# One transformer layer on one core: the forward retention states move from the attention loop into the last projection chunk, with a new order of the first instructions and of the query tiles

## The chip, the cores and the metric

The program runs on one core of a Trainium2 chip. The metric is device time in microseconds (us) of one execution; the value for a kernel is the median of its runs. PE is the matrix engine (TensorE), DVE the vector engine, ACT the scalar engine, POOL GpSimd, and SP the engine whose queue issues all DMAs here.

## The reference, cut to what matters

One layer over 2048 rows of width 1024 with a context of 256 rows. All products of activations and weights are made from pairs of float16 parts (a high and a low one, three matmuls for one), and the retention products in float32.

```python
h = modulate(rmsnorm(x)); hc = modulate(rmsnorm(ctx))
rq, rk, rv, rg, aq, ak, av = split(h @ w_in)          # 6 column chunks of w_in
# retention, 4 heads, chunks of 128 rows, forward and backward:
scores = einsum('id,jd->ij', q, k) * intra
o      = scores @ v + (q @ state) * q_dec
state  = state * c_dec + (k * k_dec).T @ v            # one update for each chunk
ret = groupnorm(o_forward + o_backward) * silu(rg)
att = softmax(q @ k_all.T) @ v_all                    # 8 query heads on 2 key heads, keys: 18 tiles of 128
x = x + g1 * (concat(ret, att) @ w_out)
x = x + g2 * (square(relu(modulate(rmsnorm(x)) @ w_ff1)) @ w_ff2)
out = rmsnorm(x) * final_norm_g
```

## The kernel before, in words

**Three stages.** A projection stage, an attention stage and a feed-forward stage follow each other. The change touches the first and the beginning of the second.

**Projection stage.** Each engine takes its instructions in the order in which the program emits them, and that order is written out by hand: `at(q, step, fn)` files a call under a half-row `q` and one of eight steps (`dma`, `mm`, `turn`, `copy`, `work`, `mix`, `extra`, `store`), and a loop at the end emits the calls by `q` and step. A row is one tile of 128 rows of activations (2 context tiles, 16 latent tiles) times one column chunk of `w_in`: 24 matmuls, 12 in each of two half-rows. The chunks come in the order value (18 rows), key (18), attention key and value (18, half as wide), attention query (16), gate (16), retention query (16). `base[col]` is the first half-row of a chunk; in the code the chunks' first half-rows are also called `rk`, `akv`, `aq`, `rg`, `rq`. Beside the rows the plan holds:

- the normalised activations, each tile once, in the value chunk (`load_x`, `squares`, `root`, `normal`, then `turn_h`, `modulate`, `high_h`, `low_h` for each half). The first tiles are made ahead of the loop, beside the modulation vectors that the first part of `w_mod` gives (`mods`, `modulation`)
- `later_rows`: the rest of the modulation vectors, on DVE, with eight float32 sums on PE
- `maxima`: the greatest weights of the later matrices, on DVE (`w_ff1`) and ACT (the others)
- `decay_tables`: the retention's decay factors, `value_parts`: the float16 parts of the values, `ff_scales`: scales for the later stages
- `first_maxima`: for the first three groups of the attention, 18 `piece` matmuls each into the PSUM tag `mp` (two buffers) and 18 `maximum` reductions on DVE

**Attention stage.** It runs over steps `k`; a list of phases (`begin`, `scores`, `piece`, `maximum`, `early`, `exp`, `cast`, `low`, `chain`, `pe`, `values`, `late`, `dma`) orders what a step emits. A group is a tile of 128 queries with one key head, 32 groups of 18 steps, from the last tile (15) to the first. A step scores one tile of keys, takes exponentials on ACT, splits them into float16 parts (ACT, then POOL or DVE) and multiplies by the values. The scores of the first group start at step 22. Group 3 is the first whose pieces and maxima are made in this stage, from step 54.

**Retention.** `retention(24)` files its work into the attention's steps. From step 24, every two steps, it makes one state: 17 forward chunks (`d` = 0), then two backward ones. For each of them `take` loads a key and a value tile of 256 KB each, `weigh` multiplies the keys by their decay on POOL, `product` makes four float32 matmuls into a PSUM bank, and `update` combines them with the old state in four DVE instructions; `keep_state` stores forward states to DRAM for later use (two buffers, tag `sf`). From step `R0` = 66, every 35 steps, one retention tile and one output tile are made.

Of the kernel before, what the change touches and what calls it, by code (L numbers as in the profile page):

```python
# [55 lines left out]
def layer_kernel(ctx: ExitStack, tc: tile.TileContext, a: dict, out: bass.AP):  # L56
# [205 lines left out]
    with ExitStack() as st:  # L262
# [212 lines left out]
        for m in range(3, len(TILES)):  # L475
            q = 2 * (m - 3)
            if m > 3:
                at(max(0, q - 6), "dma", load_x, m)
                at(max(0, q - 3), "copy", squares, m)
                at(max(0, q - 2), "work", root, m)  # L480
                at(max(1, q - 1), "mix", normal, m)
# [92 lines left out]
        class Row:  # L574


            def __init__(self, s):
# [26 lines left out]
                elif self.col == C_AQ:  # L604
# [8 lines left out]
                    at(q + 3, "turn", self.turn)  # L613
                    at(q + 4, "copy", self.split_turned)
                    at(q + 5, "store", self.store_turned, aq_d)
                else:
# [11 lines left out]
                    at(q + 6, "turn", self.turn_key)  # L628
                    at(q + 7, "work", self.keep_key)
# [301 lines left out]
        def decay_tables(q0):  # L931
# [10 lines left out]
            def rates():  # L942
# [4 lines left out]
                nc.scalar.activation(u, lr, AF.Exp)  # L947
                nc.vector.tensor_scalar(w1, u, -1.0, 1.0, op0=ALU.mult, op1=ALU.add)
                nc.scalar.activation(ln, w1, AF.Ln)
                nc.vector.tensor_scalar(z, u, -1.0, 2.0, op0=ALU.mult, op1=ALU.add)  # L950
                nc.vector.reciprocal(z, z)
                nc.vector.tensor_mul(z, z, u)
                nc.vector.tensor_mul(zz, z, z)
                nc.vector.tensor_scalar(lg, zz, 1.0 / 17, 1.0 / 15, op0=ALU.mult, op1=ALU.add)
                for k in range(13, 0, -2):
                    nc.vector.tensor_mul(lg, lg, zz)
                    nc.vector.tensor_scalar_add(lg, lg, 1.0 / k)
                nc.vector.tensor_mul(lg, lg, z)
                nc.vector.tensor_scalar_mul(lg, lg, -2.0)
                nc.vector.tensor_single_scalar(big, u, 0.5, op=ALU.is_gt)  # L960
                nc.vector.tensor_tensor(ln, ln, lg, op=ALU.subtract)
                nc.vector.tensor_mul(ln, ln, big)
                nc.vector.tensor_tensor(lg, lg, ln, op=ALU.add)
# [20 lines left out]
            at(q0 + 3, "extra", rates)  # L984
            for h in range(4):
                at(q0 + 5 + h, "extra", tables, h)
            at(q0 + 9, "extra", rest)

        def first_maxima(n, pool, tag, bufs, q_load, qs):
# [3 lines left out]
            at(q_load, "dma", g.minima, kp)  # L993
            for i, q in enumerate(qs):
# [4 lines left out]
        row_slots = [rk + 2 * i + 1 for i in range(18)] + [rg + 2 * i + 1 for i in range(14)]  # L999
# [30 lines left out]
        between = [[lambda: load_x(0), lambda: load_x(1)], [lambda: load_x(2), lambda: first.fetch(0)]]  # L1030
        between += [[lambda k=k: first.fetch(k) for k in (2, 4, 6)], [lambda: load_x(3)]]
# [18 lines left out]
        def halves_h(p, ms):  # L1050
# [161 lines left out]
    def retention(k0):  # L1212
# [93 lines left out]
        for n, (d, c) in enumerate(todo):  # L1306
# [11 lines left out]
            if d == 0 and c > 0:  # L1318
                on(k + 3, "dma", keep_state, c - 1)
# [634 lines left out]
```

## Time and profile before

| what | value |
|---|---|
| median of 3 runs | 2898.51 us (2896.85 to 2898.58) |
| the profiled execution, its own time | 2894.32 us |
| span of the profiled execution | 2892.2 us |
| busy over the span: PE, DVE, ACT, POOL | 94%, 72%, 49%, 53% |
| mean granted PE clock | 0.989 of full speed |

Times on the page and in the rows count from the span's start. A matmul's duration runs from its start to its modelled end, and matmuls overlap, so the rate at which PE takes them is read from their starts. "Idle before" is the time for which the engine had nothing to run ahead of an instruction, and the name behind the arrow is what ended it.

### The profile page before, as it was taken

The page shows a single profiled execution, that of the slowest core. Times are in us where ns is not written, and L with a number is a line of the kernel's source. Part 1 is how long each engine was busy: PE and PEld are TensorE (multiplying, and loading weights), DVE is VectorE, ACT ScalarE, POOL GpSimd, SP SyncE. Part 2 cuts the span into 40 slices and gives each one's busy share as a digit, 9 for nine tenths or more (in the row PEclk, how much of TensorE's full clock was granted, in tenths as well). Part 3 has the DMA queues.
Part 4 walks back from the last instruction along what each step waited for, and adds up shares of the span by engine and source line. Part 5 has one row for each costly group of instructions (what it writes and reads, how often), then busy time and mean ns, then how long its engine had stood idle before and what let it go on. Part 6 is the DMA issues. An engine that isn't in the chain of part 4 may idle for free. (4 is left out here: it accounts for less than half of the span.)

```text
span 2892.2 us, 45242 instructions
## 1 busy us (share of the span) xinstructions
PE 2728.7 (94%) x17152; PEld 1459.3 (50%) x17152; DVE 2094.2 (72%) x3324; ACT 1428.9 (49%) x2418; POOL 1528.8 (53%) x1289
## 2 busy tenths in 40 slices
PE   5999999988899998899999899999999999999998
PEld 2545644446566665566666344444444444444443
DVE  4556687667878777787785577777777777777776
ACT  3533762336777777777777333333333333333332
POOL 2523782338757568885667566664443434444432
PEclk8999999999999999999999999999999999999999
DMA  6478758337212213332113722231114411111111
GB/s 220 153 232 290 237 157 259 108 105 241 60 48 66 84 58 101 119 116 67 50 61 124 266 81 77 82 116 58 59 49 152 164 59 59 55 51 47 52 44 59
DMA packets 251320, 324.26 MB, mean 112 GB/s; under 512 B 106775, under 2 KB 157975, under 8 KB 249310
## 3 DMA queue, kind: packets, MB, share of 16 engines
q1 hardware_dynamic: 251102, 321.37, 34.5%
q8 instruction: 135, 2.21, 0.3%
q14 instruction: 83, 0.68, 0.1%
HBM read 249.84 MB, written 71.46 MB: 111 GB/s over the span
## 5 line engine op out<-in xcount | busy, mean ns | idle before, releaser
L180 DVE TENSOR_REDUCE nm<-mp 128x1 f32<-128x512 f32 (+1 forms) x576 | 389.5, 683 | 153.4 <-PE mp L167 124.6
L221 POOL TENSOR_TENSOR plo<-p,phi 128x1024 f16<-128x1024 f32 x160 | 353.1, 2208 | 165.6 <-ACT phi L214 136.2
L210 ACT ACTIVATE p<-st 128x512 f32<-128x512 f32 x576 | 337.8, 597 | 175.6 <-PE st L205 113.0
L1728 PE MATMUL pd<-w2hi,uhi 128*128 128x512 f16 x1024 | 388.1, 379 | 13.6 <-DVE acc L1731 13.3
L1729 PE MATMUL pd<-w2lo,uhi 128*128 128x512 f16 x1024 | 388.1, 379 | 0.6 <-DVE w2lo L72 0.6
L1730 PE MATMUL pd<-w2hi,ulo 128*128 128x512 f16 x1024 | 388.1, 379 | 0.0
L1731 DVE SCALAR_TENSOR_TENSOR acc<-pd,sc,acc 128x512 f32<-128x512 f32 x512 | 366.0, 738 | 5.7 <-PE pd L1730 5.6
L1668 PE MATMUL pu<-hf,w1f 128*128 128x512 f16 x896 | 340.3, 380 | 2.9 <-DVE q L1691 2.2
L1669 PE MATMUL pu<-hf,w1f 128*128 128x512 f16 x896 | 340.4, 380 | 0.0
L1670 PE MATMUL pu<-hf,w1f 128*128 128x512 f16 x896 | 340.2, 380 | 0.0
L214 ACT ACTIVATE phi<-p 128x1024 f16<-128x1024 f32 x288 | 303.9, 1055 | 0.0
L638 PE MATMUL pso<-whi,h 128*128 128x512 f16 (+1 forms) x816 | 294.9, 361 | 0.4 <-ACT whi L535 0.4
L639 PE MATMUL pso<-wlo,h 128*128 128x512 f16 (+1 forms) x816 | 294.5, 361 | 0.2 <-DVE wlo L536 0.2
L640 PE MATMUL pso<-whi,h 128*128 128x512 f16 (+1 forms) x816 | 294.5, 361 | 0.0
L237 PE MATMUL o<-wv,plo 128*128 128x65 f16 x2304 | 235.4, 193 | 22.9 <-POOL plo L221 16.8
L223 DVE TENSOR_TENSOR plo<-p,phi 128x512 f16<-128x512 f32 x256 | 236.1, 923 | 18.9 <-ACT phi L214 16.2
L238 PE MATMUL o<-wv,phi 128*128 128x129 f16 x2304 | 243.2, 221 | 0.0
L237 PEld LDWEIGHTS <-plo 128*128 128x128 f16 x2304 | 206.7, 98 | 57.3 <-POOL plo L221 25.6
L204 PE MATMUL st<-qr,ks 128*128 128x512 f16 x576 | 220.5, 383 | 15.1 <-ACT p L210 14.9
L1680 POOL TENSOR_TENSOR r<-r 128x512 f32<-128x512 f32 x64 | 66.3, 1039 | 295.2 <-ACT r L1679 295.2
L205 PE MATMUL st<-qr,ks 128*128 128x512 f16 x576 | 220.7, 383 | 1.1 <-DVE qr L198 1.0
L238 PEld LDWEIGHTS <-phi 128*128 128x128 f16 x2304 | 205.8, 98 | 20.0 <-issue 0.3
(326 smaller groups left out, 5393.9 us busy)
## 6 DMA issues: line engine op xcount, KB each, us to landing
wm<-in_w_ff SPq DMA_DIRECT2D x64, 512.0 KB, 5.2
w1r<-in_w_ff SPq DMA_DIRECT2D x64, 512.0 KB, 4.3
ws<-in_w_ff SPq DMA_DIRECT2D x124, 256.0 KB, 3.3
wmr<-in_w_mod SPq DMA_DIRECT2D x32, 512.0 KB, 5.5
hf<-hp SPq DMA_DIRECT2D x56, 256.0 KB, 3.2
hf<-hf SPq DMA_DIRECT2D x14, 1024.0 KB, 6.1
wst<-in_w_in SPq DMA_DIRECT2D x20, 512.0 KB, 6.1
orv<-rv SPq DMA_DIRECT2D x35, 256.0 KB, 3.0
```

The source lines that it names most:

```text
L180: nc.vector.tensor_reduce(dst, src, axis=AX.X, op=ALU.max, negate=True)
L210: nc.scalar.activation(self.p[kt // 2][:, kt % 2], self.s.pop(kt), AF.Exp, scale=HD**-0.5)
L221: nc.gpsimd.tensor_tensor(lo, p, hi, op=ALU.subtract)
L237: mm(o[:, : HD + 1], lo[:, i, c], v[:, : HD + 1], start=False, stop=False)
L238: mm(o, hi[:, i, c], v[:, :VW], start=False, stop=last)
L1668: mm(pu[i], whi, hi, start=k == 0, stop=False)
L1669: mm(pu[i], whi, lo, start=False, stop=False)
L1670: mm(pu[i], wlo, hi, start=False, stop=k == 3)
L1728: mm(ps, uh, wh, start=f == 0, stop=False)
L1729: mm(ps, uh, wl, start=False, stop=False)
L1730: mm(ps, ul, wh, start=False, stop=f == NF - 1)
L1731: nc.vector.scalar_tensor_tensor(acc[:, c], ps, sc2, acc[:, c], op0=ALU.mult, op1=ALU.add)
```

## The change

The forward states leave the attention's steps: a new function `forward_states` files them into the retention query chunk, one chunk of 128 rows about every 1.8 half-rows, from `rq + 4` on, with the tags `wm` (two buffers), `wmr` (two), `mps` (one) and `wst` (four) of earlier work. The attention keeps the two backward states, filed from step 25. Ahead of the loop, two tiles of activations are made in place of three, the loads stand in another order, and tile 2 joins the plan. The rows of the attention query chunk run from tile 15 down to tile 0, and `first_maxima` spreads over the gate chunk (groups 0 and 1) and the last chunk (group 2). The transposes of attention queries and keys stand one half-row later. `later_rows` starts in the value chunk, `decay_tables` moves to the attention key chunk and is cut into parts, `value_parts` moves to the gate chunk and `ff_scales` eight half-rows forward. The pools of the attention stage are opened in another order, which gives their tiles other addresses.

```diff
-            slots += [(n, m) for m, t in enumerate(TILES) if t[0] == "l" or col not in (C_RQ, C_RG, C_AQ)]
+            ms = [m for m, t in enumerate(TILES) if t[0] == "l" or col not in (C_RQ, C_RG, C_AQ)]
+            slots += [(n, m) for m in (ms[::-1] if col == C_AQ else ms)]
...
-        for m in range(3, len(TILES)):
-            q = 2 * (m - 3)
+        for m in range(2, len(TILES)):
+            q = 2 * (m - 2)
...
-                    at(q + 3, "turn", self.turn)
-                    at(q + 4, "copy", self.split_turned)
-                    at(q + 5, "store", self.store_turned, aq_d)
+                    at(q + 4, "turn", self.turn)
+                    at(q + 5, "copy", self.split_turned)
+                    at(q + 6, "store", self.store_turned, aq_d)
...
-                    at(q + 6, "turn", self.turn_key)
-                    at(q + 7, "work", self.keep_key)
+                    at(q + 7, "turn", self.turn_key)
+                    at(q + 8, "work", self.keep_key)
...
-            at(q0 + 3, "extra", rates)
-            for h in range(4):
-                at(q0 + 5 + h, "extra", tables, h)
-            at(q0 + 9, "extra", rest)
+            for i in range(4):
+                at(q0 + 6 + 2 * i, "extra", rates, i)
+                at(q0 + 14 + 3 * i, "extra", tables, i)
+            at(q0 + 26, "extra", rest)
+
+        def forward_states(c, q):
+
+            x = {}
+
+            def load():
+                x["k"] = sg.tile([P, 2, 512], F32, name="rkv", tag="wm")
+                for i, src in enumerate((rk_d, rv_d)):
+                    nc.sync.dma_start(x["k"][:, i], src[c])
+
+            def weigh():
+                x["w"] = sg.tile([P, 4, P], F32, name="rkw", tag="wmr")
+                k = x["k"][:, 0].rearrange("p (h d) -> p h d", h=4)
+                nc.gpsimd.tensor_tensor(x["w"], k, bc(kd[:, 0].unsqueeze(2), [P, 4, P]), op=ALU.mult)
+
+            def product():
+                x["ps"] = psM.tile([P, 4, P], F32, name="mpr", tag="mps", bufs=1)
+                for h in range(4):
+                    v = x["k"][:, 1, h * P : (h + 1) * P]
+                    mm(x["ps"][:, h], x["w"][:, h], v, start=True, stop=True)
+
+            def update():
+                old = states.get("s")
+                s = states["s"] = sg.tile([P, 4, P], F32, name="rst", tag="wst", bufs=4)
+                if old is None:
+                    nc.scalar.activation(s, x["ps"], AF.Copy)
+                    return
+                for h in range(4):
+                    nc.vector.scalar_tensor_tensor(
+                        s[:, h], old[:, h], cd[:, 0, h : h + 1], x["ps"][:, h], op0=ALU.mult, op1=ALU.add
+                    )
+
+            def store():
+                nc.sync.dma_start(sf_d[c - 1].rearrange("p (h d) -> p h d", h=4), states["s"])
+
+            at(q - 5, "dma", load)
+            at(q - 2, "mix", weigh)
+            at(q, "turn", product)
+            at(q + 1, "work", update)
+            if c > 0:
+                at(q + 1, "store", store)
...
-        row_slots = [rk + 2 * i + 1 for i in range(18)] + [rg + 2 * i + 1 for i in range(14)]
+        row_slots = [11 + 2 * i for i in range(10)] + [rk + 2 * i + 1 for i in range(18)]
+        row_slots += [rg + 2 * i + 1 for i in range(4)]
...
-        value_parts(aq + 4)
-        decay_tables(rq)
-        ff_scales(rq + 13)
-        first_maxima(0, xp, "x", 4, rg + 8, [rg + 13 + i for i in range(18)])
-        first_maxima(1, sg, "wst", 4, rq, [rq + 4 + i * 12 // 17 for i in range(18)])
-        first_maxima(2, sg, "wst", 4, rq + 10, [rq + 17 + i * 12 // 17 for i in range(18)])
+        decay_tables(akv)
+        value_parts(rg + 2)
+        ff_scales(rq + 5)
+        states, end = {}, base["end"]
+        for c in range(NK - 1):
+            forward_states(c, rq + 4 + c * 29 // 16)
+        first_maxima(0, hp, "h0", 1, aq + 20, [rg + i * 16 // 18 for i in range(NK)])
+        first_maxima(1, hp, "h1", 1, aq + 24, [rg + 16 + i * 16 // 18 for i in range(NK)])
+        first_maxima(2, hp, "h0", 1, rg + 20, [rq + 2 + 2 * i for i in range(14)] + [end, end, end + 1, end + 1])
...
-        between = [[lambda: load_x(0), lambda: load_x(1)], [lambda: load_x(2), lambda: first.fetch(0)]]
-        between += [[lambda k=k: first.fetch(k) for k in (2, 4, 6)], [lambda: load_x(3)]]
+        between = [[lambda: load_x(0), lambda: load_x(1)], [lambda k=k: first.fetch(k) for k in (0, 2)]]
+        between += [[lambda k=k: first.fetch(k) for k in (4, 6)], [lambda: load_x(2), lambda: load_x(3)]]
...
-        modulation(2, (ready, 2), (halves_h, 0, (0,)), (first.bound, 0), (halves_h, 0, (1,)))
+        modulation(2, (first_half, 0), (first.bound, 0), (first_half, 1), (first.bound, 2))
         mods[2].end()
         mods[2].shift_and_scale()
-        modulation(3, (halves_h, 0, (2,)), (first.bound, 2), (first.bound, 4), (first.bound, 6))
+        modulation(3, (first.bound, 4), (first.bound, 6))
         turn_h(0, 1)
         mods[3].end()
         mods[3].shift_and_scale()
         first.greatest()
+        modulate(0, 1)
         first.spread()
-        modulate(0, 1)
+        turn_h(1, 1)
         first.scales()
+        first.split(0)
         high_h(0, 1)
         low_h(0, 1)
-        first.split(0)
         first.split(2)
-        halves_h(1, (1,))
+        modulate(1, 1)
         first.split(4)
+        high_h(1, 1)
+        low_h(1, 1)
         first.split(6)
-        halves_h(1, (2,))
-        ready(3)
+        ready(2)
...
-    qp = pool(attn, "qp")
-    op = pool(attn, "op2", 2)
-    vp = pool(attn, "vp")
     pp = pool(attn, "pp", 3)
+    op = pool(attn, "op2", 2)
+    qp = pool(attn, "qp")
+    vp = pool(attn, "vp")
...
-        SF = 2
-        todo = [(0, c) for c in range(NK - 1)] + [(1, 1), (1, 0)]
-        for n, (d, c) in enumerate(todo):
-            k = k0 + SF * n
+        for n, c in enumerate((1, 0)):
+            k = k0 + 2 * n
...
-    retention(24)
+    retention(25)
```

## Rows read from the trace of the kernel before

**Rows 1.** Windows: us, busy us (instructions) of each engine, PE clock, DMA share, GB/s.

```profile
0.00:68.00 68.00, 36.10 (x195) 14.56 (x196) 29.33 (x95) 23.46 (x46) 13.51 (x25) 0.82 0.65 218
68.00:172.00 104.00, 101.25 (x523) 52.98 (x522) 54.60 (x87) 55.38 (x102) 46.51 (x55) 1.00 0.45 148
...
276.40:334.20 57.80, 52.92 (x473) 46.06 (x472) 31.24 (x105) 45.04 (x108) 33.08 (x78) 1.00 0.79 247
...
427.10:523.50 96.40, 93.21 (x428) 41.12 (x427) 75.96 (x109) 25.50 (x48) 27.43 (x23) 1.00 0.75 237
523.50:628.00 104.50, 98.27 (x485) 48.38 (x483) 67.90 (x158) 28.38 (x52) 33.19 (x38) 1.00 0.28 89
632.00:706.00 74.00, 62.69 (x573) 47.59 (x572) 48.48 (x110) 51.59 (x82) 55.97 (x37) 0.90 0.79 248
```

**Rows 2.** Timeline around 62 us: start, us, engine, line, operation, idle time before.

```profile
61.73 0.75 DVE L450 TENSOR_SCALAR x_l<-x_l,ry_x 128x1024 f32<-128x1024 f32 x1 [1.26 <-POOL ry_x L81]
...
62.63 1.09 PE L459 MATMUL psx<-ident,x_l 128*128 128x128 f32 x4 [10.51 <-DVE x_l L450]
```

**Rows 3.** Windows at half clock, and one of thin PE work.

```profile
56.10:66.30 10.20, 3.67 (x11) 1.92 (x12) 6.17 (x16) 4.23 (x8) 4.07 (x6) 0.50 0.00 0
...
677.30:684.10 6.80, 5.67 (x31) 4.64 (x32) 4.38 (x11) 3.42 (x6) 4.52 (x4) 0.50 0.92 280
725.00:749.00 24.00, 17.62 (x182) 10.81 (x181) 20.14 (x38) 19.45 (x34) 18.60 (x15) 1.00 0.28 86
```

**Rows 4.** What PE waited for, 276.4 to 334.2 and 334.2 to 427.1: us, times, longest.

```profile
PE psx L741 <- DVE kn L736: 4.5, 5, 1.4
...
PE psx L691 <- DVE ys L723: 2.5, 2, 1.7
```

**Rows 5.** Timeline of PE from 640.1 us: a state product between two scores.

```profile
640.14 0.38 PE L205 MATMUL st<-qr,ks 128*128 128x512 f16 x1
640.36 0.61 PE L1235 MATMUL bank<-orv,okw 128*128 128x128 f32 x4
641.01 0.38 PE L204 MATMUL st<-qr,ks 128*128 128x512 f16 x1
```

**Rows 6.** Groups of instructions, 523.5 to 628.0: busy us, mean ns, idle before.

```profile
L167 PE MATMUL mp<-ks,qr 128*128 128x512 f16 x32 | 10.9, 379 | 1.8 <-DVE nm L180 1.8
...
L180 DVE TENSOR_REDUCE nm<-mp 128x1 f32<-128x512 f32 (+1 forms) x36 | 23.8, 683 | 0.5 <-PE mp L167 0.4
...
L974 ACT ACTIVATE tf<-rel,dw 128x128 f32<-128x128 f32 x4 | 1.5, 386 | 0.0
...
L972 ACT ACT_TABLE_LOAD x1 | 1.3, 1283 | 0.0
```

**Rows 7.** Groups of instructions, 632 to 706.

```profile
L1235 PE MATMUL bank<-orv,okw 128*128 128x128 f32 x152 | 26.4, 301 | 6.6 <-POOL okw L1229 6.6
...
L1229 POOL TENSOR_TENSOR okw<-ork,kd 128x512 f32<-128x512 f32 x17 | 20.3, 1196 | 7.3 <-DMA ork<-rk 7.0 <-POOL okw L1229 0.3
...
L1245 DVE SCALAR_TENSOR_TENSOR sf<-sf,cd,bank 128x128 f32<-128x128 f32 x64 | 18.8, 341 | 24.2 <-DMA sf<-sf 13.4 <-PE bank L1235 10.5
```

**Rows 8.** What ACT waited for, 632 to 706.

```profile
ACT wo L1377 <- POOL wos L1372: 10.6, 3, 7.1
ACT p L210 <- PE st L205: 8.0, 14, 1.5
```

**Rows 9.** Timeline of ACT: two casts of one steady stretch.

```profile
640.85 1.05 ACT L214 ACTIVATE phi<-p 128x1024 f16<-128x1024 f32 x1
...
642.75 1.06 ACT L214 ACTIVATE phi<-p 128x1024 f16<-128x1024 f32 x1
```

**Rows 10.** Timeline between the stages: last transpose's input, first group's maxima turned.

```profile
626.77 1.51 DVE L686 TENSOR_TENSOR ys<-t,t 128x512 f32<-128x512 f32 x1 [1.29 <-POOL t L674]
...
631.15 1.12 PE L191 MATMUL mp<-ident,mt 128*128 128x128 f32 x4 [2.10 <-POOL mt L1121]
```

**Rows 11.** DMA issues, 632 to 706: KB each, median us to landing.

```profile
ork<-rk SPq DMA_DIRECT2D x16, 256.0 KB, 4.4
```

More of the change, by code (lines that the diff above doesn't have):

```diff
@@ L940, in load, with rates @@
                 nc.sync.dma_start(w[:, 8:10], a["pos"])
-            def rates():
+            def rates(part):
                 w = x["w"]
@@ L946, in rates @@
                 x["lg"] = lg
[L947 to L963, printed above, removed]
+                if part == 0:
+                    nc.scalar.activation(u, lr, AF.Exp)
+                    nc.vector.tensor_scalar(w1, u, -1.0, 1.0, op0=ALU.mult, op1=ALU.add)
+                    nc.scalar.activation(ln, w1, AF.Ln)
+                    nc.vector.tensor_scalar(z, u, -1.0, 2.0, op0=ALU.mult, op1=ALU.add)
+                    nc.vector.reciprocal(z, z)
+                    nc.vector.tensor_mul(z, z, u)
+                    nc.vector.tensor_mul(zz, z, z)
+                    nc.vector.tensor_scalar(lg, zz, 1.0 / 17, 1.0 / 15, op0=ALU.mult, op1=ALU.add)
+                elif part < 3:
+                    for k in ((13, 11, 9, 7), (5, 3, 1))[part - 1]:
+                        nc.vector.tensor_mul(lg, lg, zz)
+                        nc.vector.tensor_scalar_add(lg, lg, 1.0 / k)
+                else:
+                    nc.vector.tensor_mul(lg, lg, z)
+                    nc.vector.tensor_scalar_mul(lg, lg, -2.0)
+                    nc.vector.tensor_single_scalar(big, u, 0.5, op=ALU.is_gt)
+                    nc.vector.tensor_tensor(ln, ln, lg, op=ALU.subtract)
+                    nc.vector.tensor_mul(ln, ln, big)
+                    nc.vector.tensor_tensor(lg, lg, ln, op=ALU.add)
             def tables(h):
@@ L993, in first_maxima @@
             at(q_load, "dma", g.minima, kp)
+            assert len(qs) == NK
             for i, q in enumerate(qs):
@@ L1302, in gated @@
             rets[c] = o.rearrange("p h d -> p (h d)")
-        SF = 2
-        todo = [(0, c) for c in range(NK - 1)] + [(1, 1), (1, 0)]
-        for n, (d, c) in enumerate(todo):
-            k = k0 + SF * n
+        for n, c in enumerate((1, 0)):
+            k = k0 + 2 * n
             on(k - 5, "dma", take, c, "rk", "rv")
-            on(k - 2, "late", weigh, d, c)
-            on(k, "pe", product, c, n % 2, (0, 1))
-            on(k + 1, "pe", product, c, n % 2, (2, 3))
-            if d == 0:
-                old, to, tag = None if c == 0 else ("s", c - 2), ("s", c - 1), "sf"
-            else:
-                old, to, tag = None if c == 1 else ("b", NT), ("b", NT - 1 + c), "sb"
-            on(k + 1, "late", update, d, c, old, to, tag, (0, 1))
-            on(k + 2, "late", update, d, c, old, to, tag, (2, 3))
-            if d == 0 and c > 0:
-                on(k + 3, "dma", keep_state, c - 1)
-        assert k0 + SF * len(todo) + 2 <= R0
+            on(k - 2, "late", weigh, 1, c)
+            on(k, "pe", product, c, n, (0, 1))
+            on(k + 1, "pe", product, c, n, (2, 3))
+            old = None if c == 1 else ("b", NT)
+            on(k + 1, "late", update, 1, c, old, ("b", NT - 1 + c), "sb", (0, 1))
+            on(k + 2, "late", update, 1, c, old, ("b", NT - 1 + c), "sb", (2, 3))
         for n in range(NT):
@@ L1788, in layer_kernel @@
     with tc.manual_schedule():
-        for k in range(min(events)[0], max(made_at + 1, last) + 1):
+        for k in range(min(events)[0], max(events)[0] + 1):
             for phase in PHASES:
```

16 lines of the change are left out of this document (6 added, 10 removed).

## The prediction

> **What bounds the kernel now.** I read first the busy time by windows, one window for each chunk of the projection stage and one for the attention steps 22 to 66, then what PE and ACT waited for in them, then single stretches of the timeline.
>
> In the last projection chunk PE is the bound. A 512-column matmul takes 0.216 us from start to start (640.14 to 640.36, [rows 5]), so a row of 24 takes 5.2 us, and 16 rows 83 us. With 16 transposes of four blocks at about 0.4 and 36 pieces at 0.216 that is 97 us, which is what PE shows busy of 104.5 [rows 1, 6]. The gate chunk is nearly as dense (93.2 of 96.4, DVE 76.0). The attention key chunk has two engines near the top: PE 52.9 and ACT 45.0 of 57.8 [rows 1]. The first 68 us are loads and chains: PE is busy for 36.1, and the first row of the plan stands still for 10.51 us until tile 3 is normalised [rows 1, 2].
>
> Steps 22 to 66 are another case. They take 74 us, and no engine is full: PE 62.7, ACT 51.6, POOL 56.0, DVE 48.5 [rows 1]. ACT sets the pace where nothing is late: two casts, with the exponentials of two steps between, stand 1.90 us apart [rows 9], 42 us for 44 steps. What is late are the states: DVE waits 13.4 us until a stored state has landed and its buffer is free, POOL 7.0 for keys, PE 6.6 for weighed keys [rows 7], and ACT, behind all of them, 10.6 for POOL and 8.0 for scores [rows 8].
>
> **The change part by part.** The sum is made against the profiled execution (2894.3: its span of 2892.2 and 2.1 around it). The median of the runs is 4.2 higher, which I add at the end.
>
> *Start.* Fewer instructions stand ahead of the tile that the first row's transposes wait for (tile 2 now, the second half of the old third tile no longer ahead of it), and ACT's bounds of the first weights no longer stand behind that tile. The splits of the weights still do. Bounds: the wait stays whole, or all 10.5 us go [rows 2]. Two transposes of tile 2 move from a stretch in which PE waits for loads into rows that it bounds: +0.8 (eight blocks at about 0.10, the spacing of a state product's parts, below). PE still idles for some microseconds there, so half clock, as now from 56.1 to 66.3 [rows 3], stays likely. I take half the wait, -5.3, and +0.8: -4.5.
>
> *Transposes half a row later.* They remove PE's waits for keys (4.5) and queries (2.5) [rows 4]. Against the first stands the next edit.
>
> *Decay tables in the attention key chunk.* ACT gets three table loads at 1.28 and some 12 exponentials at no more than 0.39 [rows 6], 8.5 us on top of 45.0 in a chunk of 57.8 that PE needs 52.9 of. ACT's idle 12.8 covers it if it falls in the right places; if none does, the chunk grows by 8.5. What waits behind ACT there is the split of the keys, the same chain that PE waited for. Chunk as a whole: -2, between -4.5 and +4; queries -2.5. Two more table loads come with it, back for the gate's Silu and again for the attention's first exponential: 1.28 each, the first hidden (ACT is busy for 25.5 of 96.4 [rows 1]), the second on the way to the first product of scores: +0.5. The Trainium skill (ScalarE: Activation LUTs, What ACT_TABLE_LOAD costs) says that a switch of sets costs 2.66 us with its drain and should be batched; the profile shows the load alone, and by the page the two extra switches would take 5.3 us of ACT in place of 2.6.
>
> *Maxima, `later_rows`, values, scales.* Twenty-two pieces leave the last chunk, 18 go to the gate chunk and 4 behind the last row, where PE idles: -0.9. PE's waits for their reductions (1.8) go. In the gate chunk DVE gains 18 reductions at 0.683, 12.3 us on 76 of 96.4 [rows 1, 6], and loses ten of its additions. Its eight sums on PE stay in chunks that PE bounds. The value chunk takes the additions on DVE (54.6 of 104). I take -1 for the gate and last chunk's waits (from -1.8 to +4) and +1 for the value chunk (0 to +4).
>
> *States in the last chunk.* Sixteen of 17 products fall between rows that PE bounds. In the attention, half of one took 0.65 us between two scores [rows 5], 1.30 for all; the lower end is eight records about 0.10 apart (four end within 0.61, one is 0.30 long [rows 5, 7]), 0.83. In one block the extra gap comes once, so 0.95: +15.2, between 13.3 and 20.8. POOL (33 of 104.5 busy) takes 17 weighings at 1.2, DVE 68 updates at 0.34 in place of 22 reductions at 0.68 (67.9 busy [rows 1, 6, 7]), SP 34 loads and 16 stores at a DMA share of 0.28: hidden. Behind a load that waits stand on SP the rope tables and stores of later rows, due three and two half-rows later.
>
> *Between the stages.* After the last rope addition ends at 628.28, DVE now has four reductions and one update (four instructions), 2.7 + 1.4 us, before it reaches the first group's maxima. Their transposes at 631.15 waited 2.10 for POOL's memset, which other addresses free [rows 10]. Net +2, from 0 to +4.
>
> *Attention, steps 22 to 66.* Nineteen products become two; with them go the state waits. Lower end: only PE's 6.6 for weighed keys go. Upper end: the stretch falls to ACT's busy 51.6, -22.4. Both of ACT's waits gone (18.6) would leave 55.4. The output weights still need POOL and loads, and the first steps still run at half clock, so I take 58: -16. It is nearer to the upper end because the waits of DVE, POOL and PE have all one source, and it leaves.
>
> Sum: -4.5 + 0.5 - 2 - 2.5 - 0.9 - 1 + 1 + 15.2 + 2 - 16 = -8.2. That is 2886.1 for the profiled execution and **2890 us** for the median.
>
> **The rivals.**
>
> *More is won.* The start's whole wait goes and the attention comes down to ACT's busy time: -5.2 and -6.4 more, -19.8, 2879. For it: ACT's dense stretches [rows 9]. Against it: half clock behind both gaps.
>
> *It evens out.* ACT's wait of 10.6 is for POOL's gated output weights [rows 8], and if these are late by their own loads, the attention gives back about 7, the last chunk still pays 15: sum about +1, 2899. A second way to the same time is the clock. With 17 products gone (26.4 us for 19 [rows 7]) PE is busy for about 39 of 58 us. It fell to half at 677.3, after a wait of several microseconds, but stayed at full from 725 to 749 with PE busy for 17.6 of 24 [rows 3]. Twenty microseconds at half would add 7 (20 × 39/58 × half). The Trainium skill (TensorE: Matmul & The Clock Gate, HAM oscillation) warns that gaps between bursts throttle the array again; by that rule the thinner stretch would lose part of its gain, while the trace shows a stretch nearly as thin at full clock.
>
> *Slower.* The states' keys and values have two buffers, so the load of chunk c waits for the product of c - 2, and SP, in order, waits with it. Landing 4.4 [rows 11], weighing 1.2, and POOL's rope work ahead of it (33.2 us over 16 rows, 2 a row) make 8 us; two chunks have 3.6 half-rows of 3.3, 11.8. From 11.8 on PE pays the excess eight times: at 14 us +18, total +10, 2908 with the offset. For it: keys landed late in the attention, POOL waited 7.0 for them; against it: DMA was at 0.79 there and is at 0.28 here.
>
> **How the numbers follow.** Forecast 0.43, more won 0.20, evened out 0.25 (0.05 of it by the clock), slower 0.12. The forecast's own range is 2880 to 2897. The range for all, 2872 to 2904, takes the bounds of start and attention on one side, and even plus the cheaper half of slower on the other. A measurement of this kernel tells about 0.2% (5.8 us) from no change. Faster by more: 0.36 of the forecast, all of more won, 0.03 of evened out, 0.59. Within: 0.07 + 0.20 + 0.01, 0.28. Slower: 0.02 + 0.11, 0.13.
>
> **What would show it.** The value chunk's rows in step some 5 us before 68; no wait of PE for key or query transposes; a last chunk about 8 to 11 us longer than 104.5 (products in, pieces out), with no PE wait for weighed keys; the first scores some 2 us further behind the last row; steps 22 to 66 in about 58 us, no DVE wait for a stored state. Wrong if PE waits in the last chunk, if the key chunk grows with ACT full, or if the attention's first 44 steps stay near 70.

## The result, and the profile after

The change makes the kernel slower: 2906.07 us median of 7 runs (2903.94 to 2909.19) against 2896.85 of the kernel before, a ratio of 1.0032 with a 95% interval of 1.0020 to 1.0044. The profiled execution took 2903.94 us, its span 2902.1. The forecast was 2890 us and faster.

The table lays the two profiles side by side. A projection chunk counts from the first matmul of its first row to that of the next chunk (the value chunk from its second row), the last one to the end of its last matmul; the feed-forward part counts from the last product of scores to the end of the span.

| stretch, us | before | after | difference | forecast |
|---|---|---|---|---|
| up to the second row | 67.9 | 60.4 | -7.5 | -4.5 |
| value chunk from there | 104.1 | 111.3 | +7.1 | +1 |
| key chunk | 104.4 | 104.9 | +0.5 | 0 |
| attention key and value chunk | 57.7 | 64.5 | +6.8 | -2 |
| attention query chunk | 93.0 | 89.7 | -3.3 | -2.5 |
| gate and last chunk | 196.4 | 211.7 | +15.3 | +13.3 |
| last row to first scores | 8.5 | 9.1 | +0.6 | +2.5 |
| attention steps 22 to 66 | 74.1 | 59.8 | -14.3 | -16 |
| rest of the attention | 871.1 | 868.8 | -2.3 | 0 |
| feed-forward part | 1315.0 | 1321.9 | +7.0 | 0 |
| sum | 2892.2 | 2902.1 | +9.9 | -8.2 |

Between the forecast's sum and the measured one lie 18.1 us. Three rows miss it by 8.8 (attention key and value chunk), 7.0 (feed-forward part) and 6.1 (value chunk); the others together are 3.8 better than forecast.

Windows of the changed kernel, with the columns of [rows 1]: the value chunk, the attention key chunk, the gate chunk, the last chunk, and steps 22 to 66.

```profile
60.40:171.70 111.30, 106.14 (x537) 54.48 (x535) 77.58 (x113) 56.61 (x105) 49.75 (x59) 0.98 0.60 187
276.60:341.10 64.50, 55.47 (x474) 47.12 (x473) 37.32 (x138) 51.46 (x127) 33.80 (x80) 0.97 0.72 226
430.70:530.80 100.10, 95.75 (x442) 43.74 (x441) 75.33 (x116) 29.82 (x54) 23.97 (x21) 0.98 0.59 187
530.80:642.50 111.70, 107.72 (x578) 60.04 (x576) 64.62 (x157) 19.52 (x31) 48.00 (x48) 0.98 0.52 172
651.70:711.50 59.80, 47.02 (x436) 28.31 (x437) 33.15 (x50) 51.46 (x83) 39.56 (x25) 0.91 0.40 116
```

Three things are to be read here. In the attention's steps ACT is now at 51.5 of 59.8 us, the nearest to full of the engines, as forecast. In the attention key chunk ACT has gone from 45.0 [rows 1] to 51.5, and the chunk has grown by about as much. And the value, attention key and gate chunks, all at full clock before [rows 1], show 0.97 and 0.98. What PE waited for in three of these chunks (value, attention key, gate), in us, times, longest:

```profile
PE psx L460 <- DVE x_l L451: 2.8, 3, 1.8
PE mps L387 <- DVE macc L382: 2.2, 2, 1.5
...
PE psx L743 <- DVE kn L738: 7.5, 4, 2.8
...
PE mp L167 <- DVE nm L180: 3.8, 3, 2.5
```

The first two lines are the value chunk's. The timeline of DVE there shows what stands ahead of the normalised tile and behind it (start, us, engine, line, operation):

```profile
112.66 0.90 DVE L516 COPY wmb<-wm 128x128 f32<-128x128 f32 x1
113.48 0.74 DVE L451 TENSOR_SCALAR x_l<-x_l,ry_x 128x1024 f32<-128x1024 f32 x1
114.14 1.53 DVE L382 SCALAR_TENSOR_TENSOR macc<-wmr,cc,macc 128x512 f32<-128x512 f32 x2
```

and PE behind it:

```profile
114.36 0.63 PE L460 MATMUL psx<-ident,x_l 128*128 128x128 f32 x4 [1.81 <-DVE x_l L451]
115.72 1.07 PE L387 MATMUL mps<-macc,ones 128*32 128x512 f32 x2 [0.73 <-DVE macc L382]
```

PE waits 1.81 us for the tile, then for the additions (L382), and runs one of their sums, two records in 1.07. What stands ahead of the tile is a copy (L516), not an addition: in the run below that takes the additions out of this chunk, PE still waits 1.38 at this place. The additions make PE wait for themselves, ahead of their sums. The third line of the waits is the attention key chunk's. ACT's timeline there is that of the decay tables ahead of a key's high part (`kh`, L737):

```profile
304.65 0.19 ACT L820 ACTIVATION_READ_ACCUMULATOR junk<-wm 128x1 f32 x1
304.86 1.28 ACT L977 ACT_TABLE_LOAD   x1
306.15 0.31 ACT L977 ACTIVATE dT<-dw 128x128 f32<-128x128 f32 x1
306.37 0.39 ACT L979 ACTIVATE tf<-rel,dw 128x128 f32<-128x128 f32 x1
306.66 0.39 ACT L980 ACTIVATE tb<-rel,dw 128x128 f32<-128x128 f32 x1
306.95 0.29 ACT L737 ACTIVATE kh<-kn 128x128 f16<-128x128 f32 x1
```

with PE at its end:

```profile
307.84 0.66 PE L743 MATMUL psx<-ident,kn 128*128 128x128 f32 x2 [2.61 <-DVE kn L738]
```

Behind some of these waits the clock falls. Windows of the changed kernel right behind one wait in the value, attention key, gate and last chunks:

```profile
116.60:120.00 3.40, 3.40 (x9) 1.19 (x9) 1.59 (x4) 1.67 (x3) 1.78 (x3) 0.50 0.76 224
...
307.80:311.20 3.40, 3.36 (x16) 2.53 (x17) 1.88 (x7) 2.69 (x8) 2.13 (x6) 0.51 0.19 55
512.60:516.00 3.40, 3.40 (x10) 1.22 (x8) 2.29 (x3) 0.00 (x0) 0.00 (x0) 0.51 0.13 30
584.20:587.60 3.40, 3.40 (x10) 1.20 (x9) 3.12 (x9) 0.00 (x0) 0.00 (x0) 0.50 0.46 116
```

PE is busy all through them at half rate, so each gives away half of 3.4, 1.7 us (worked out from these rows). The longest wait of the attention key chunk is not followed by such a stretch:

```profile
329.50 0.41 PE L743 MATMUL psx<-ident,kn 128*128 128x128 f32 x2 [2.83 <-DVE kn L738]
329.60:333.00 3.40, 3.40 (x32) 3.07 (x33) 2.30 (x10) 3.27 (x10) 1.65 (x5) 1.00 0.86 241
```

So half clock is counted below only where rows show it.

The wait in the last chunk is that of a state product. DVE and POOL first, then PE:

```profile
580.63 0.89 DVE L890 SCALAR_TENSOR_TENSOR sc<-sc,fsb 128x1 f32<-128x1 f32 x1
...
582.05 1.11 DVE L1021 SCALAR_TENSOR_TENSOR rst<-rst,cd,mpr 128x128 f32<-128x128 f32 x4
...
580.43 1.07 POOL L1006 TENSOR_TENSOR rkw<-rkv,kd 128x512 f32<-128x512 f32 x1 [2.60 <-DMA rkv<-rk]
```

```profile
548.06 1.05 PE L1012 MATMUL mpr<-rkv,rkw 128*128 128x128 f32 x8
548.95 0.38 PE L640 MATMUL pso<-whi,h 128*128 128x512 f16 x1
...
576.33 1.13 PE L1012 MATMUL mpr<-rkv,rkw 128*128 128x128 f32 x8 [1.22 <-issue]
577.30 0.38 PE L640 MATMUL pso<-whi,h 128*128 128x512 f16 x1
...
583.25 1.15 PE L1012 MATMUL mpr<-rkv,rkw 128*128 128x128 f32 x8 [2.77 <-issue]
```

A product costs 0.89 in a dense row (548.06 to 548.95), as 12 of the 15 ahead of the chunk's last matmul do, and 0.97 behind a wait (576.33 to 577.30); the forecast had 0.95 for 16. But the product at 583.25 starts when the update of the one before ends (582.05 + 1.11): the states have one PSUM bank, and the update stands on DVE behind the scales of the later stages (L854 to L890). Its weighed keys were there only at 581.50 (580.43 + 1.07), since their load came late, so of the 2.77 us about 1 is the load's in any case. Ahead of the first scores, PE waited 2.82 us for the first group's maxima, behind the four reductions on DVE; the memset of [rows 10] no longer shows.

### The profile page after: what moved, and what is told of

Same layout as the page of the kernel before. It is cut to its first block, busy times and chain, and to the rows that moved or that the text cites. A ratio compares the mean times of both kernels' runs of the same rounds, so it can differ in the third digit from the quotient of the medians.

```text
span 2902.1 us, 45253 instructions
## 1 busy us (share of the span) xinstructions
PE 2734.2 (94%) x17152; PEld 1456.4 (50%) x17152; DVE 2100.7 (72%) x3324; ACT 1430.6 (49%) x2419; POOL 1518.7 (52%) x1289
## 6 DMA issues: line engine op xcount, KB each, us to landing
hf<-hf SPq DMA_DIRECT2D x14, 1024.0 KB, 13.6
```

## The experiments

Each ratio is to the kernel before, timed in the same comparison, and where two of them are set against each other the difference carries the uncertainty of both.

**The pools in the old order.** The changed kernel with

```diff
-    pp = pool(attn, "pp", 3)
-    op = pool(attn, "op2", 2)
     qp = pool(attn, "qp")
+    op = pool(attn, "op2", 2)
     vp = pool(attn, "vp")
+    pp = pool(attn, "pp", 3)
```

> The changed kernel with the attention's pools opened in the old order again. Overlay theory: in the changed kernel the feed-forward part, from the last score to the end, is 7.0 us longer than before (1321.9 against 1315.0), because its first tiles of activations got addresses that come free later, so that their loads meet the last store of the attention's rows; with the old order it is 1314 to 1317, the wait of POOL for that store is back near 5 us from 8.7, and the time falls by 5 to 7, to about 2900. Rival, the loss there is that execution's chance: the feed-forward part stays within 2 us of what the changed kernel shows, or the time does not move (2904 to 2908).

Measured: 2900.87 us, ratio 1.0014 (1.0005 to 1.0022); feed-forward part 1314.5. At its beginning POOL normalises tiles of activations in place, and waits until their stores have landed (changed kernel, then this one; the first tile's own wait is 8.7 and 3.9):

```profile
POOL xr L1486 <- DMA x<-xr: 14.0, 2, 8.7
...
SPq L1696 <- DVE r L247: 7.3, 1, 7.3
```

```profile
POOL xr L1486 <- DMA x<-xr: 9.3, 2, 5.4
...
SPq L1696 <- DVE plo L223: 3.6, 1, 3.6
```

L1696 issues the feed-forward's activation loads, seven of 1 MB each. In the new order six of them come out from 1590.0 on, behind a wait of 7.3 us for a reciprocal of the attention's last group. In the old order two come out at 1586.5 and 1586.9, behind 3.6, and the other four from 1591.8 on. Meanwhile the DMA engines are busy for 0.22 of the time in the new order and all the time in the old one (changed kernel, then this one, columns of [rows 1]):

```profile
1587.50:1592.00 4.50, 3.66 (x18) 1.56 (x16) 1.68 (x3) 2.17 (x6) 4.42 (x6) 1.00 0.22 67
1589.30:1593.80 4.50, 3.66 (x18) 1.56 (x16) 1.68 (x3) 2.22 (x7) 4.42 (x6) 1.00 1.00 417
```

The first tile's store is issued at 1599.26 and 1601.03. The last of the loads lands 10.3 and 5.6 us behind it, and POOL starts 1.5 and 1.4 us later still, 11.8 and 7.0 us after the store's issue. That the order of the pools does this is shown. That the store waits behind the late loads is read from these landings, and was not tried by itself.

**The pools alone**, the mirror of it: the kernel before with the new order and nothing else.

> The kernel before with the new order of the attention's pools alone. Overlay theory: the projection stage is as before, the feed-forward part grows by 5 to 7 (from 1315 to 1320 to 1322), and the time rises by 4 to 7, to 2900 to 2903. Rival, the longer feed-forward part needs the rest of the change (its shorter attention or other tiles): within 2 us of before.

Measured: 2899.3 us, ratio 1.0004 (0.9995 to 1.0013); feed-forward part 1321.4. The profile shows the loss whole, and PE's longest wait behind POOL's `xr` is 6.6 us as in the changed kernel; the gap ahead of the first scores is 2.1 us shorter (6.5), since the memset's wait goes. Net that is some 4 us by the profile, of the slowest of 11 executions, and 1.2 us by the ratio, with an interval up to 3.8: the theory's time was missed low, and by the time alone the rival would hold. Over all profiles of this study the feed-forward part is 1319.8 to 1322.6 in the five with the new order and 1313.4 to 1318.9 in the eleven with the old, and PE's waits for `xr` there are 10.1 to 10.8 against 5.0 to 6.4.

**The later modulation rows back in the gate chunk.**

```diff
-        row_slots = [11 + 2 * i for i in range(10)] + [rk + 2 * i + 1 for i in range(18)]
-        row_slots += [rg + 2 * i + 1 for i in range(4)]
+        row_slots = [rk + 2 * i + 1 for i in range(18)] + [rg + 2 * i + 1 for i in range(14)]
```

> The changed kernel with the later modulation rows back at their old places (key chunk and gate chunk, none in the value chunk). Theory of the full cover: the value chunk paid 7.1 us for additions on DVE that stand ahead of a tile's normalisation; without them it falls from 111.3 to 104 to 106, PE waits there for DVE go, the gate chunk gains 1 to 4 for ten additions more, and the time falls by 2 to 5, to 2901 to 2904. Rival, the value chunk is longer because it starts earlier and now makes tile 2 itself, and the first rows have less lead: it stays at 109 or more and the time is 2905 to 2909.

Measured: 2906.51 us, ratio 1.0036 (1.0022 to 1.0050). The value chunk falls to 105.6 at full clock, as expected, but the gate chunk grows to 107.9:

```profile
61.00:166.60 105.60, 102.43 (x533) 53.85 (x531) 57.35 (x92) 56.45 (x105) 49.77 (x59) 1.00 0.45 145
424.90:532.70 107.80, 99.79 (x451) 44.03 (x450) 91.32 (x138) 29.84 (x54) 23.90 (x21) 0.97 0.74 223
```

DVE is at 91.3 of 107.8 there. Right for the value chunk, wrong for the price of the other place; the time lies in the rival's range, but its reason, a value chunk of 109 or more, is out. In the value chunk PE's waits fall from 5.0 to 3.2; at the tile shown above they fall little:

```profile
113.56 0.63 PE L460 MATMUL psx<-ident,x_l 128*128 128x128 f32 x4 [1.38 <-DVE x_l L451]
```

**The decay tables in the query chunk.**

```diff
-        decay_tables(akv)
+        decay_tables(aq)
```

> The changed kernel with the decay tables in the attention query chunk in place of the attention key chunk. Theory of the full cover: ACT is at 53 of 66 us in the key chunk, and the table loads and exponentials stand ahead of the keys' high parts, for which PE waits; without them the key chunk falls from 64.5 to 53 to 56 (also below the 57.7 of before, whose waits for keys the later transposes take away), the query chunk grows by 0 to 4 from 89.7, and the time falls by 5 to 10, to 2896 to 2901. Rival, the later transposes of the keys or DVE's own work are what makes the key chunk longer: it stays above 61 and the time falls by less than 3.

Measured: 2897.17 us, ratio 1.0002 (0.9993 to 1.0011). The attention key chunk falls to 56.6, PE's waits for keys there from 7.5 to

```profile
PE psx L743 <- DVE kn L738: 1.1, 3, 0.6
```

and the query chunk takes the tables at no cost (89.65 in both), with ACT at 65 of 90. The rival is out. Of the 7.9 us that the chunk gives back, 6.1 are PE's waits (9.0 to 2.9 in all) and 1.7 the half-clock stretch.

**The states back in the attention.** The changed kernel without `forward_states`, with the old loop over all 19 states:

```diff
-        for c in range(NK - 1):
-            forward_states(c, rq + 4 + c * 29 // 16)
...
+        todo = [(0, c) for c in range(NK - 1)] + [(1, 1), (1, 0)]
```

> The changed kernel with the forward states back in the attention's steps, as before; all the rest as changed. Theory that the states' move is about even in itself: the last chunk falls from 111.7 to 94 to 98 (products at about 0.97 each, and the waits for the products' one bank), the attention's steps 22 to 66 grow from 59.8 to 73 to 76, and the time stays within 3 us of the changed kernel's, 2903 to 2909. Rival, the states' move is what makes the kernel slower: the last chunk gives back 5 us or more beyond what the attention takes, and the time falls to 2901 or less. Second rival, the move is a gain hidden by other losses: the time rises to 2911 or more.

Measured: 2900.93 us, ratio 1.0022 (1.0011 to 1.0032); last chunk 92.0 (-19.7), steps 22 to 66 75.6 (+15.8). The time falls on the edge of the first rival, and the chunk gives back 3.9 beyond what the attention takes, less than that rival's 5: this one run did not decide.

**Two mends together**: old pools and decay tables in the query chunk.

> The changed kernel with two mends together: the old order of the attention's pools, and the decay tables in the query chunk. If the two losses stand in series (each delays the end by its own amount), the time is that of the changed kernel less both, 5 and 9 us: 2890 to 2894 where before is 2896.5, a ratio of 0.998 to 0.9995. Rival, one slack pays for both: 2896 or more.

Measured: 2891.8 us, ratio 0.9985 (0.9976 to 0.9993), faster than before. The two losses stand in series. Against the run with the decay tables alone moved, the pools are again worth 5 us (1.0002 to 0.9985).

**The later rows in the query chunk as well.**

```diff
+        row_slots = [rk + 2 * i + 1 for i in range(18)] + [aq + 2 * i + 9 for i in range(10)]
+        row_slots += [rg + 2 * i + 1 for i in range(4)]
```

> The same two mends, and the ten additions of later modulation rows that stood in the value chunk moved to the attention query chunk, where DVE is busy for 73 of 90 us and PE waits for nothing. Theory of the cover: the value chunk falls from 112 to 105 to 107, the query chunk grows by 0 to 2 and the gate chunk stays at 100 to 101 (in the run that moved them to the gate chunk it grew by 8): 3 to 6 us faster than with two mends alone, 2885 to 2890. Rival, DVE's total over the stage is what counts and the additions cost the same wherever they stand: the query chunk grows by 5 or more and the time does not move.

Measured: 2897.23 us, ratio 1.0005 (0.9996 to 1.0013). The value chunk falls to 105.6, and the query chunk grows from 89.65 to 101.8, for which my theory had 0 to 2:

```profile
327.60:429.40 101.80, 95.31 (x459) 45.86 (x457) 89.67 (x166) 65.21 (x129) 77.69 (x91) 0.98 0.70 217
```

What PE waited for in it:

```profile
PE mps L387 <- DVE macc L382: 4.2, 3, 1.4
PE psx L306 <- issue: 2.3, 1, 2.3
```

DVE's 72 us of 90 were room on average. No transpose of a query waits; PE waits for the additions themselves, ahead of their three sums. These waits (6.5), the sums and the turn of their rows on PE (3.4), and one stretch at half clock (1.7) make 11.6 of the 12.1 us. The rival's times hold, and its reason, DVE's total, does not.

**The later rows spread**, on the two mends: six at the end of the value chunk, four in the attention key chunk, and the products on the pieces' two banks.

```diff
+        row_slots = [30 + i for i in range(6)] + [rk + 2 * i + 1 for i in range(18)]
+        row_slots += [akv + 6 + 8 * i for i in range(4)] + [rg + 2 * i + 1 for i in range(4)]
```

> The changed kernel with the two mends, the state products on the pieces' two banks, and the ten additions of later modulation rows where DVE has room: six in the last six half-rows of the value chunk, behind the last normalisation, and four in the attention key chunk (DVE 32 of 57 us). Theory that the place and not the total of DVE's work decides: value chunk 105 to 107, key chunk of the retention 105 to 106, attention key chunk 56 to 59, query chunk 90, last chunk 108 to 110: 4 to 8 us faster than the two mends alone, 2884 to 2888. Rival, each addition costs PE its own time wherever it stands, as in the query chunk (12 us for ten): 2891 or more.

Measured: 2902.6 us, ratio 1.0017 (1.0007 to 1.0026); value chunk 109.4, attention key chunk 69.0. There DVE, with 39 us of work in 69, stood still for the additions' own weights, and the keys queued behind them:

```profile
DVE kn L738 <- ACT kh L737: 8.5, 9, 2.7
DVE macc L380 <- DMA wmr<-in_w_mod: 6.5, 1, 6.5
```

The rival's time holds. In the changed kernel no place that was tried takes the ten additions for less than the value chunk did.

**Two banks for the state products**, on the three mends (pools, decay tables, rows in the query chunk):

```diff
-                x["ps"] = psM.tile([P, 4, P], F32, name="mpr", tag="mps", bufs=1)
+                x["ps"] = psM.tile([P, 4, P], F32, name="mpr", tag="mp")
```

> The three mends, and the state products take the two PSUM banks of the maxima's pieces in place of one bank of their own. If the single bank makes products wait for the update of the one before while DVE works on the later stages' scales, PE's waits ahead of the products (4.0 us in the changed kernel) go and the last chunk is 2 to 5 us shorter than with one bank, 104 to 107. Rival, the pieces between the products use the same two banks and wait for DVE in their place, or the wait is for weighed keys: the last chunk within 1.5 us or longer.

Measured: 2896.62 us, ratio 1.0002 (0.9994 to 1.0011); last chunk 109.6 from 112.4: 2.8 shorter, as the theory had it, but above its 104 to 107. The window of the chunk is at full clock now, from 0.98: the stretch at half clock, 1.7, is gone, and PE's waits fall only from 4.5 to 3.7. What PE still waits for in it:

```profile
PE mp L167 <- DVE rst L1021: 1.6, 1, 1.6
PE mpr L1012 <- POOL rkw L1006: 1.4, 1, 1.4
PE mpr L1012 <- issue: 0.7, 1, 0.7
```

Pieces now wait for updates and a product for weighed keys, as the rival said, and the gap ahead of the first scores grows by 1.8: no gain in the time. Two runs with one bank have a last chunk that is shorter still, also at full clock: 108.7 with the rows back in the gate chunk, and 108.4 with the decay tables moved alone. So what the bank itself costs is not shown.

**The three mends without the states' move.**

> The three mends with the forward states back in the attention's steps: against the three mends alone this prices the move of the states by itself. Theory that the move is about even: the last chunk falls by 16 to 20 (to 90 to 93), steps 22 to 66 grow by 14 to 17 (to 73 to 77), and the time is within 4 us of the three mends with the states in the chunk, 2882 to 2890. Rival, the move is a real gain once the other losses are gone: this run is 6 us slower or more, 2892 and above. Second rival, the move is the larger loss: 6 us faster or more, 2880 or less.

Measured: 2894.52 us, ratio 0.9991 (0.9982 to 1.0000), 2.7 less than the same with the move; last chunk 92.0 (-20.3), steps 22 to 66 78.5 (+18.0). The times of the expectation took the three mends to be faster than they are (2897.23); against that run it is the theory's "within 4 us".

**The two mends without the states' move.**

> The changed kernel with the two mends (old order of the pools, decay tables in the query chunk) and the forward states back in the attention. Beside the two mends alone (2891.8) it prices the move of the states once more. Theory that the move costs PE in the last chunk a little more than the attention gives back: last chunk 92, steps 22 to 66 at 73 to 79, and 2 to 4 us faster than the two mends, 2887 to 2891. Rival, the move is a gain: 2894 or more.

Measured: 2890.68 us, ratio 0.9978 (0.9969 to 0.9987). Its last chunk and its steps 22 to 66, and these steps in the two mends with the move:

```profile
527.40:619.40 92.00, 92.00 (x458) 45.62 (x456) 44.04 (x101) 19.36 (x30) 28.50 (x31) 1.00 0.24 82
627.50:706.10 78.60, 62.57 (x574) 47.81 (x572) 49.63 (x113) 53.72 (x85) 58.65 (x40) 0.89 0.77 248
645.60:706.60 61.00, 46.98 (x438) 28.49 (x437) 33.30 (x49) 50.70 (x82) 38.76 (x23) 0.92 0.36 107
```

Without the products PE has no gap in the last chunk. Back in the attention they make PE busy for 15.6 us more, and the steps 17.6 longer: PE's gaps there were 14.0 without them and are 16.0 with them. The thin stretch did not hide the products, and the dense one paid waits on top. That is the trade.

**The start and the later transposes alone**, in the kernel before.

> The kernel before with two parts alone: the new order of the first instructions, and the transposes of queries and keys one half-row later. Theory that these are the sound parts of the change: first row 6 us earlier, value chunk +1.5 (tile 2 joins the plan), key chunk -1 to -2.5, query chunk -2 to -3.3, the rest unchanged: 8 to 11 us faster than before, 2885 to 2889, a ratio near 0.9965. Rival, the microseconds won at the start are given back later, at a stage that waits for loads or stores: 2893 or more.

Measured: 2888.77 us, ratio 0.9975 (0.9966 to 0.9984), the lowest time of the study, with an interval that overlaps that of the run before (0.9969 to 0.9987). Second row at 60.7, value chunk +1.5, attention key chunk -2.2, query chunk -3.3, as expected, the gate chunk 1.6 longer; by the medians 9.0 us less than before, in the expected range, with a ratio on the weak side of it. The profile alone would speak for the rival. It is of the slowest of ten executions, its span is 2892.8, and what the projection stage wins is given back behind it: steps 22 to 66 are 4.5 longer, at a lower clock than before [rows 1], the rest of the attention 1.9 and the feed-forward part 4.0.

```profile
622.30:700.90 78.60, 65.55 (x573) 50.27 (x572) 49.26 (x110) 52.02 (x83) 55.47 (x38) 0.85 0.73 234
```

The median is 6.1 us below this execution, so most executions keep more of the gain.

**The attention values' float16 parts earlier**, on the two mends, with the states in the last chunk and without:

```diff
-        value_parts(rg + 2)
+        value_parts(aq + 24)
```

> The changed kernel with the two mends (old order of the pools, decay tables in the query chunk), and the values' float16 parts ten half-rows earlier, so that on DVE they no longer stand among the splits of the next weights. Theory that the place makes the wait: PE's 2.5 us wait ahead of a maximum and the half clock behind it go, the gate chunk falls from 101.2 to 97 to 98.5, and the time falls by 2 to 4, to 2888 to 2890. Rival, the 18 maxima more fill DVE: the gate chunk stays at 100 or more, the waits stand elsewhere in it, and the time does not move.

> The same with the forward states back in the attention. If the gate chunk gives its 3 us here too and the states' move is about even, 2885 to 2890, a ratio of 0.996 to 0.9975; if the maxima fill DVE, the time is that of the run without the states, 2890.7, within 2 us.

Measured: 2894.36 us, ratio 0.9993 (0.9984 to 1.0002), and 2892.55, ratio 0.9986 (0.9978 to 0.9995); gate chunk 102.2 and 102.3, from 101.2 and 100.8. My theory falls: PE's wait only changes its place (5.0 us for an addition of the later rows, 2.1 for a maximum). The gate chunk takes 18 pieces, 3.9 us at 0.216 [rows 5], and has lost three of its four float32 sums, some 3 us: PE's own work in it is nearly what it was, and its growth is in the main waits and half clock.

## Why the prediction was wrong

*Start* (-4.5; -7.5 up to the second row, of which the value chunk gives back 1.5 with tile 2): right in mechanism, low in size. More of the 10.5 us went than the half that I took.

*Transposes half a row later, query side* (-2.5; -3.3): right, also by themselves in the kernel before. PE waits for nothing in that chunk.

*Decay tables in the attention key chunk* (-2 for the chunk; +6.8): this step failed. I let ACT's idle 12.8 us cover most of 8.5 and named +4 as the end. The chunk is a chain (ACT splits a key, DVE takes the rest, PE turns it) with two engines near full, and a table load and three exponentials in one block, 2.1 us, stand ahead of one key. PE's waits in the chunk rose to 9.0 in place of falling, and half clock stood behind one of them. With the tables elsewhere the later transpose gave -0.4 to -2.3, near the forecast's -2 at best; the smaller gains are those of the runs in which one of the later rows' sums (0.98 on PE) had moved into this chunk.

*`later_rows` in the value chunk* (+1, at most +4; +7.1): this step failed too. I read DVE's busy 54.6 of 104 [rows 1] as cover. The 5.7 us that the run with the rows back in the gate chunk gives back are, by the rows, two float32 sums of 1.0 on PE, 1.8 of waits (5.0 against 3.2) and 1.7 of half clock. The other 1.5 is tile 2. I had written that the sums stay in chunks that PE bounds, and so counted them as nothing: two of them had moved into this one, where PE also waits for their additions.

*The pools* (only a memset's wait; +5 to +7 in the feed-forward part): the step that is missing. I priced the new addresses where the profile showed a wait on them, in the gap between the stages, and did not ask which later tiles would lie on them. It cost some 5 us in both pairs that differ in the pools alone and hold the rest of the change. In the kernel before, the feed-forward part grew by as much, and the net of both ends was too small to tell by the time.

*States in the last chunk* (+15.2; 19.5 to 20.3 in four pairs): the product's price was nearly right (0.89 to 0.97), and 15 of them stand in the chunk, 13.6 us. The rest of the 19.7 is 4.0 of PE's waits ahead of two products and 1.7 of half clock behind the longer one, within some tenths. That wait stood behind the single bank and DVE's scales, and in part behind a late load. The prediction let DVE's 68 updates hide (64 in the program; the first state is a copy on ACT); each hides as long as no product waits for it. The rival of SP's loads came only in small: POOL waited 10.6 us for keys in seven waits in the changed kernel, and in five other runs PE waited once, for 1.3 to 1.6, for weighed keys. It never paid the forecast's eight times.

*Maxima* (-1.9 for pieces and waits; in the four runs without the states, gate and last chunk together stand at 190.8 to 194.3 against 196.4, -5.6 to -2.1): right in direction, but not by its own terms. Three sums that left the gate chunk, which the prediction counted as staying, are some 3 us of it, and in the changed kernel PE's waits in the gate chunk rose from 3.2 to 4.2.

*Between the stages* (+2.5; +0.6): inside its bounds, low. *Attention* (-16; -14.3 between the two profiles, 15.8 to 18.8 in the four pairs with and without the states): right. The rival of the clock did not come: steps 22 to 66 ran at 0.91 of full clock, against 0.90 before [rows 1].

So the move that gives the change its name is about even, with a small loss. The four pairs give 2 to 4 us to the side without it (2.9, 4.1, 2.0 and 2.0 by the ratios, 5.1, 2.7, 1.1 and 1.8 by the medians), each with intervals that overlap, and all in one direction. The gain at the start is real, and was spent in three places: the additions and their sums in the value chunk, the tables on ACT in the attention key chunk, and the addresses in the feed-forward part. Undoing two of them alone makes the change a gain (2891.8).

What stays open: whether the store at the head of the feed-forward part would land in time if the loads alone came out earlier, what the products' one bank costs by itself, and where the ten additions would cost nothing. The new order of the query tiles and the spread of the maxima were not run by themselves; the query chunk is as long without the new order (89.7 with the start and the later transposes alone) as with it.

## What to carry to other kernels

Idle time of an engine in a dense stretch is cover only if the added block fits between two items of the chain that the bound engine waits for: ask what is the next thing queued behind the block and when it is due, and whether the bound engine waits for the block itself, not what share is idle. When work moves between stages, count everything that PE runs for it, and ask of every reordered buffer which later tile takes its address. And try the parts of a bundled change one by one: here two small parts alone (0.9975) beat the whole (1.0032).

## What the runs showed of the hardware

Single waits of PE of 1.8 to 2.8 us inside otherwise dense work were followed by 3.4 us at half clock in the four places shown, so such a wait can cost more than its length. It need not: the wait of 2.83 us at 329.50 was followed by full clock. So was, in the run with two banks, the same wait of 2.48 us in the gate chunk that half clock follows in the changed kernel (the changed kernel, then the two banks with the window behind it):

```profile
512.02 0.38 PE L167 MATMUL mp<-ks,qr 128*128 128x512 f16 x1 [2.48 <-DVE nm L180]
...
511.84 0.38 PE L167 MATMUL mp<-ks,qr 128*128 128x512 f16 x1 [2.48 <-DVE nm L180]
511.90:515.30 3.40, 3.40 (x17) 1.51 (x17) 3.04 (x5) 0.00 (x0) 0.41 (x1) 1.00 0.22 83
```

The Trainium skill (TensorE: Matmul & The Clock Gate, HAM oscillation) describes a clock that throttles again in waits between bursts of work; the trace agrees, for some single waits too and not for all.

A switch of ACT's tables took 1.3 us here: the instruction before it ends at 304.84, the load takes 1.28, and the exponential starts at 306.15. No drain beside it shows in these rows; the 2.66 us of the Trainium skill (ScalarE: Activation LUTs, What ACT_TABLE_LOAD costs) do not fit them, and for this kernel the measured time holds.

Where no engine is waited for, the duration of a projection chunk agrees between executions to some tenths (the query chunk 89.65 in ten profiles). Where PE waits it does not: with the same program in them the value chunk took 111.3 to 112.9 us in eight profiles, and the last chunk 108.4 to 112.4 in seven. The time of the kernel before ran from 2888.9 to 2902.8 us over the comparisons. So a stage table told apart parts that the total could not, down to some 2 to 4 us in the chunks with waits.
